# Eight-step chunks and float32 matmuls in a state-space layer and in neighbourhood attention

## The chip, the cores and the metric

One core of a Trainium2 chip runs the whole kernel as one launch. The metric is the device time of that launch in microseconds (us), as the median of the timed runs. Engines are called as the profile does: PE (matmul), PEld (its weight loads), DVE (vector), ACT (scalar), POOL (GpSimd) and SP (which issues most DMAs).

## The reference, cut to what matters

One layer over 512 latent tokens and 256 context tokens of width 1024. A combined projection feeds a convolution branch, a state-space branch and an attention branch; their outputs are gated, merged and projected, and an MLP follows. Everything is float32.

```python
def s5_latent_states(ux, s5p, h0_f, h0_b):        # 32 groups of 16 channels, 64 complex states, two directions
    h_f = diag_scan(lam_bar[0], s5_drive(ux, b_bar[0])) + jnp.exp(lam_dt[0] * steps) * h0_f[:, None]
    h_b = diag_scan(lam_bar[1], jnp.flip(s5_drive(ux, b_bar[1]), 1)) + jnp.exp(lam_dt[1] * steps) * h0_b[:, None]
    return h_f, jnp.flip(h_b, 1)
...
def s5_output(u, h_f, h_b, c_mat, d_skip, w_glu_a, w_glu_b):
    y = jnp.real(jnp.einsum('blgp,gnp->blgn', h_f, c_mat[0]) + jnp.einsum('blgp,gnp->blgn', h_b, c_mat[1]))
    y = y.reshape(u.shape).astype(u.dtype) + d_skip * u
    g = jax.nn.gelu(y)
    return (g @ w_glu_a) * jax.nn.sigmoid(g @ w_glu_b)
...
    # attention, 8 heads of 64: each grid row of 64 queries sees a window of 8 x 16 and all 256 context keys
    s_loc = jnp.einsum('bqhd,bwkhd->bhqwk', q_r, k_r).astype(jnp.float32) * scale + bias
    s_loc = jnp.where(key_in[:, None, :], s_loc, NEG_INF)
    s_ctx = jnp.einsum('bqhd,bchd->bhqc', q_r, kch).astype(jnp.float32) * scale
    p = jax.nn.softmax(jnp.concatenate([s_loc.reshape(...), s_ctx], axis=-1), axis=-1)
    return jnp.einsum('bhqwk,bwkhd->bqhd', p_loc, v_r) + jnp.einsum('bhqc,bchd->bqhd', p[..., n_loc:], vch)
```

The scan has a period: over a chunk of some steps the state is multiplied by a power of lam_bar and gets a sum of the inputs of these steps, so it can be run over chunks, with small matrices for what goes on within one.

## The kernel before

Large products are made of **units** (list in `unit_list`, line 37): cg and xb (convolution), uc (context input of the state-space layer), ga, cv, gb, gc (gates and convolution output), q, k, v, then lb, la (GLU of the state-space layer), na (attention output), wo and the MLP's m1 and m2. A unit has 1 MB or half of it of weights; blocks of two halves stream from DRAM on SP's queue (`fetch`, 130; two blocks ahead). To keep float32 accuracy each operand is split into two reduced-precision parts (F32R), hi and lo: ACT casts, DVE subtracts (`wsplit`, 161; `split`, 90), and a product is three matmuls, hi-hi, hi-lo and lo-hi (`mm3`, lines 99 to 101). A unit is 24 matmuls of 512 columns; k and v have 24 more of 256 columns for the context; uc has 24 of 256.

`slot` (1172) makes one unit: it splits the weights of the unit two places on, pumps the **generators** that are open (a piece of side work each), makes half of the products, pumps again and makes the other half. The framework then orders the instructions of each engine from a simulated timeline; the state-space generator has high priority (`ahead`). Generators: `gen_par` (230), powers of the state-space parameters on [128, 32] tiles; `gen_ctx` (506); `gen_mod` (1128), late modulation columns on POOL, ACT and DVE; then `gen_s5a`, `gen_s5b` and attention.

**S5A** (`gen_s5a`, 528) runs in eight batches of four groups. With chunks of four steps it makes the matrices E (inputs to chunk states) and CA (states to outputs), 256 wide for a batch; six products or sums each on POOL and DVE (`prod`, 536). E goes to DRAM, E and the masked C are split, and 16 short matmuls per batch (580, 581) give lag matrices (kps, kev). At the end these go through DRAM twice to become Toeplitz blocks: KF_d and KB_d are written, read as kf and kb (600), added on POOL (603) and written as K_d.

**S5B** (class at 612, `gen_s5b` at 758) moves pairs of groups through a pipeline, two pieces to a step, 16 pairs. Piece A: `load` (E and, every second pair, u in eight DMAs), `load2` (CA, K), `scan` of the pair before (four scans of 192 chunks: 64 of context, 128 of latent tokens), `states` (12 split matmuls of 192 columns), `transp` (E transposed on PE), `back1`, `rot1`, `back2`. Piece B: `rot2`, `outp` of two pairs before (18 split matmuls of 128 columns; the K part uses 64 rows), then the splits of E and u, the sine `table`, and the splits of h, CA and K. DVE does scans, rotations and lo parts; POOL rr, v, h and one lo part; ACT casts and sines. Results go to Y_d in DRAM.

**Attention** (class at 798) works on four pairs of heads times four tiles of 128 queries. Its pool of tiles needs the memory of S5B, so S5B must be through: the run (1218 to 1237) lets it end before q1, and q0, k0 and v0 may lie beside its last steps. `scores` (830) takes hi and lo of k stacked on 128 rows against doubled q, then a 64-row matmul for q's lo part: eight matmuls a tile. DVE adds the bias (842) and takes the maximum (843), ACT the exponential (850), DVE scales, PE transposes eight blocks (863), ACT and DVE split them (pth, ptl), and `values` (869) needs 24 matmuls with 64-wide weights, both heads on output partitions 0 to 63.

Of the kernel before, what the change touches and what calls it, by code (L numbers as in the profile page):

```python
# [53 lines left out]
def stream_list():  # L54
    """Halves in the order in which they are read: start, then units with the late modulation tiles."""
# [20 lines left out]
def trunk(tc, xT, ctxT, cond, vecs, wst, s5p, s5bc, dmat, biasA, outT):  # L76
# [5 lines left out]
    def f(ap):  # L82
        return ap.bitcast(F32)
# [20 lines left out]
    with es:  # L104
# [120 lines left out]
        # =====================================================================  # L225
        # S5: parameters, then per batch of four groups E, CA and the lag matrices
        # =====================================================================
        s5 = {}

        def gen_par(pool, keep):  # L230
            n_sl = [0]
            prm = pool.tile([128, 40, G], F32, name="prm")
# [48 lines left out]
            pr, pi = [None] * 5, [None] * 5  # L281
            pr[1], pi[1] = sl(), sl()
            V.tensor_tensor(pr[1], r1, cs, op=MUL)
            V.tensor_tensor(pi[1], r1, sn, op=MUL)
            ph = keep.tile([128, G], F32, name="ph")
            V.tensor_scalar(ph, tht, 4.0 * 0.15915494309189535, None, op0=MUL)
            V.tensor_scalar(k, ph, ROUND, ROUND, op0=ADD, op1=SUB)
            V.tensor_tensor(ph, ph, k, op=SUB)
            r4 = keep.tile([128, G], F32, name="r4")
            V.tensor_tensor(r4, r1, r1, op=MUL)  # L290
            V.tensor_tensor(r4, r4, r4, op=MUL)
            yield

            t1, t2 = sl(), sl()

            def cmul(orr, oi, ar, ai, br, bi):
                V.tensor_tensor(t1, ai, bi, op=MUL)
                V.tensor_tensor(t2, ai, br, op=MUL)
                V.tensor_tensor(orr, ar, br, op=MUL)
                V.tensor_tensor(oi, ar, bi, op=MUL)  # L300
                V.tensor_tensor(orr, orr, t1, op=SUB)
                V.tensor_tensor(oi, oi, t2, op=ADD)

            for i, (x, y) in {2: (1, 1), 3: (2, 1), 4: (2, 2)}.items():
                pr[i], pi[i] = sl(), sl()
                cmul(pr[i], pi[i], pr[x], pi[x], pr[y], pi[y])
                yield
            # q = (lam_bar - 1) / lam
            den, nr, qr, qi = sl(), sl(), sl(), sl()
# [4 lines left out]
            V.tensor_scalar(nr, pr[1], 1.0, None, op0=SUB)  # L314
            V.tensor_scalar(t2, lim, -1.0, None, op0=MUL)
            yield
            nl = sl()
            V.tensor_copy(nl, t2)
            cmul(qr, qi, nr, pi[1], lre, nl)
            V.tensor_tensor(qr, qr, den, op=MUL)  # L320
            V.tensor_tensor(qi, qi, den, op=MUL)
            yield
            dr, di = [qr], [qi]
            for i in range(1, 4):
                dr.append(sl())
                di.append(sl())
                cmul(dr[i], di[i], qr, qi, pr[i], pi[i])
                yield
            CF = {n: keep.tile([128, G, 4], F32, name="CF" + n) for n in ("cr", "nci", "ncr", "ar", "ai")}
            for s in range(4):  # L330
                for lo_, hi_, e, c in ((0, 64, 3 - s, s + 1), (64, 128, s, 4 - s)):
                    sel = slice(lo_, hi_)
# [279 lines left out]
        class S5B:  # L612
# [37 lines left out]
            def transp(self, q):  # L650
                ps = pa(f"etps{q}")[:, :256].rearrange("p (c m) -> p c m", c=2)
                for c in range(2):
                    PE.transpose(ps[:, c], self.t["eb", q][:, c], ident)
# [840 lines left out]
```

## Time and profile before

| what | us |
|---|---|
| timed runs (three), lowest, median, highest | 1111.8, 1113.29, 1119.03 |
| the profiled execution: span from the first to the last instruction | 1117.5 |
| PE busy in the span | 1028.6 (92%) |
| DVE busy | 749.1 (67%) |
| ACT busy | 473.8 (42%) |
| POOL busy | 324.2 (29%) |

The profiled execution has no time of its own apart from its span, which is 4 us above the median of the timed runs. A busy PE is not PE at its peak: matmuls overlap, so start-to-start distances tell the rate, and durations don't. PEclk is the granted clock of PE as a share of full speed.

### The profile page before, as it was taken

To read this page: it belongs to the slowest core of one execution; us is meant where nothing else is said; L and a number is where in the kernel's file an instruction comes from. 1 tells how busy PE (TensorE), PEld (TensorE's weight loads), DVE (VectorE), ACT (ScalarE), POOL (GpSimd) and SP (SyncE) were. 2 spreads that over 40 slices of the span, in tenths; PEclk is the share of its full clock that TensorE was granted. 3 is DMA by queue.
4 is the path that set the end of the run, shared out by engine and by line. 5 is a ranking of instruction groups with operands and counts; after the bars stand their busy time and mean duration, and the time that the engine had idled before them with its cause. 6 is when DMAs were issued, how large, how long until landed. Compare 5 with 4: busy or idle time off the path is not lost.

```text
span 1117.5 us, 14237 instructions
## 1 busy us (share of the span) xinstructions
PE 1028.6 (92%) x5350; PEld 848.0 (76%) x5350; DVE 749.1 (67%) x1084; ACT 473.8 (42%) x843; POOL 324.2 (29%) x254
## 2 busy tenths in 40 slices
PE   4669978989898898899999999999999999999997
PEld 3448777767676676777887778899888888888887
DVE  8999899628979989977658787756443223443322
ACT  5336543216444535545556554434432112433211
POOL 2771565216877878761010010000000000000000
PEclk9789989998888898899999999999999999999999
DMA  7544156395334353333224355522232323232202
GB/s 267 188 188 151 49 196 217 125 139 182 103 90 142 120 163 133 137 126 138 97 98 146 132 187 172 215 76 81 109 113 76 113 76 113 79 110 88 101 1 76
DMA packets 62760, 142.81 MB, mean 128 GB/s; under 512 B 18194, under 2 KB 40978, under 8 KB 50212
## 3 DMA queue, kind: packets, MB, share of 16 engines
q1 hardware_dynamic: 60788, 138.75, 37.8%
q10 hardware_dynamic: 1904, 3.16, 0.9%
q8 instruction: 42, 0.69, 0.2%
q14 instruction: 26, 0.21, 0.1%
HBM read 125.96 MB, written 15.93 MB: 127 GB/s over the span
## 4 chain that ended last, share of the span: by engine, by line
PE 58%; POOL 9%; DVE 7%; DMA 3%; issue 3%; SPq 2%; ACT 1%; DVEq 0%; POOLq 0%; ACTq 0%
PE m L99 10%; PE m L100 10%; PE m L101 10%; DVE v L711 2%; PE sps L840 2%; POOL v L703 2%; PE ptps L863 1%; PE sps L839 1%; PE wo L100 1%; PE wo L99 1%; PE wo L101 1%; POOL h L726 1%; PE ops L99 1%; POOL h L723 1%; POOL h L725 1%
## 5 line engine op out<-in xcount | busy, mean ns | idle before, releaser
L174 DVE TENSOR_TENSOR wl<-raw,wh 128x1024 fp32r<-128x1024 f32 x144 | 188.9, 1313 | 142.5 <-ACT wh L171 140.6
L171 ACT CAST wh<-raw 128x1024 fp32r<-128x1024 f32 x144 | 150.7, 1047 | 251.1 <-PE m L100 151.1
L99 PE MATMUL m<-rg,wh 128*128 128x512 f32 (+1 forms) x480 | 184.2, 385 | 0.0
L101 PE MATMUL m<-rg,wl 128*128 128x512 f32 (+1 forms) x480 | 183.9, 384 | 0.0
L101 PEld LDWEIGHTS m<-rg,wl 128*128 128x128 f32 x480 | 90.1, 188 | 19.0
L99 PEld LDWEIGHTS m<-rg,wh 128*128 128x128 f32 x480 | 90.0, 188 | 18.7
L100 PE MATMUL m<-rg,wh 128*128 128x512 f32 (+1 forms) x256 | 96.4, 378 | 0.0
L100 PE MATMUL m<-actl,wh 128*128 128x512 f32 x224 | 87.8, 392 | 0.0
L1134 POOL TENSOR_TENSOR junk<-raw,silx 128x1024 f32<-128x1024 f32 x16 | 43.0, 2684 | 138.3 <-DMA raw<-in_wst_dram 138.3
L711 DVE TENSOR_TENSOR_SCAN v<-r,v 128x192 f32<-128x192 f32 x64 | 53.5, 882 | 10.0 <-POOL v L703 7.5
L438 POOL TENSOR_TENSOR prod<-raw,silc 128x1024 f32<-128x1024 f32 x16 | 47.1, 2968 | 35.0 <-ACT prod L447 23.5
L100 PEld LDWEIGHTS m<-rg,wh 128*128 128x128 f32 x256 | 48.0, 188 | 8.6
L100 PEld LDWEIGHTS m<-actl,wh 128*128 128x128 f32 x224 | 42.0, 188 | 9.8
L1089 DVE SCALAR_TENSOR_TENSOR fg<-m,mod,fg 128x512 f32<-128x512 f32 x14 | 10.5, 752 | 52.8 <-PE m L101 52.8
L92 ACT CAST rg<-relu 128x512 fp32r<-128x512 f32 (+1 forms) x36 | 20.3, 575 | 38.6 <-DVE relu L1082 38.6
L93 DVE TENSOR_TENSOR actl<-relu,rg 128x512 fp32r<-128x512 f32 (+1 forms) x36 | 22.3, 633 | 18.5 <-ACT rg L92 18.5
L723 POOL TENSOR_TENSOR h<-A 64x256 f32<-64x256 f32 x16 | 19.7, 1231 | 44.1 <-DVE A L717 44.1
L92 ACT CAST hh<-h 128x512 fp32r<-128x512 f32 x16 | 9.9, 618 | 52.8 <-POOL h L726 52.7
L100 PE MATMUL wo<-rg,wh 128*128 128x256 f32 (+1 forms) x104 | 32.0, 309 | 0.0
L436 DVE SCALAR_TENSOR_TENSOR junk<-raw,silx 128x1024 f32<-128x1024 f32 x16 | 31.8, 1988 | 0.0
L101 PE MATMUL wo<-rg,wl 128*128 128x256 f32 (+1 forms) x104 | 31.7, 306 | 0.0
L99 PE MATMUL wo<-rg,wh 128*128 128x256 f32 (+1 forms) x104 | 31.6, 307 | 0.0
(484 smaller groups left out, 2943.6 us busy)
## 6 DMA issues: line engine op xcount, KB each, us to landing
raw<-in_wst_dram SPq DMA_DIRECT2D x94, 1024.0 KB, 4.9
E_d<-e SPq DMA_DIRECT2D x8, 512.0 KB, 2.9
u<-U_d SPq DMA_DIRECT2D x64, 48.0 KB, 2.1
fg<-in_xT_dram SPq DMA_DIRECT2D x4, 512.0 KB, 5.8
raw<-in_wst_dram SPq DMA_DIRECT2D x4, 512.0 KB, 7.4
U_d<-un SPq DMA_DIRECT2D x4, 512.0 KB, 3.8
bc<-in_s5bc_dram ACTq DMA_DIRECT2D x8, 256.0 KB, 3.0
eb<-E_d SPq DMA_DIRECT2D x16, 128.0 KB, 2.8
```

Of the source, the lines that this page charges most:

```text
L92: S.copy(hi, src)
L99: PE.matmul(ps, a[0], b[0], start=start, stop=False)
L100: PE.matmul(ps, a[0], b[1], start=False, stop=False)
L101: PE.matmul(ps, a[1], b[0], start=False, stop=stop)
L171: S.copy(a, src)
L174: V.tensor_tensor(b, src, f(a), op=SUB)
L436: jins[d] = V.scalar_tensor_tensor(junk, w, 1.0, silx, op0=MUL, op1=MUL, accum_out=modx[:, h[1]:h[1] + 1])
L438: P.tensor_tensor(pr, w, silc, op=MUL)
L703: P.tensor_tensor(v[:, :, 0], A[:, :, 0], A[:, :, 1], op=SUB)
L711: V.tensor_tensor_scan(v[:, g, c], r4, v[:, g, c], 0.0, op0=MUL, op1=ADD)
L723: P.tensor_tensor(h[0:64, 0], A[0:64, :, 0], A[0:64, :, 1], op=ADD)
L1134: P.tensor_tensor(junk, half(h), silx, op=MUL)
```

## The change

**State-space layer.** Chunks have eight steps instead of four, so there are 32 + 64 = 96 of them instead of 192, and groups go through S5B by four instead of two: eight steps. All its matmuls take float32 operands directly; the splits are gone. `gen_par` makes powers 1 to 8 in wider operations. S5A's products are twice as wide; PE transposes E there, before E_d is written. The lag matrices are written once, to one table KT_d, from which each step reads its Toeplitz block. u is stored forward only; the backward direction reads it with a negative step, as a second matmul into the right half of the array (output partitions 64 to 127).

**Attention.** q, k, v and the probabilities stay float32. A head's scores use its own 64 rows of q and k, so the two heads use the upper and lower half of the array's rows; in `values` they use the left and the right half of its columns. The bias tile has zeros for the context keys, and one DVE instruction adds and takes the maximum. S5B now has to end before q0.

```diff
@@ gen_s5a
+                e1 = pool.tile([128, 2, 512], F32, tag="e1", bufs=2, name=f"e1{b}")
+                c1 = pool.tile([128, 2, 512], F32, tag="c1", bufs=1, name=f"c1{b}")
...
+                nc.sync.dma_start(C_d[b], c1)
                 yield
-                ebh = pool.tile([128, 512], F32R, tag="ebh", name=f"ebh{b}")
-                ebl = pool.tile([128, 512], F32R, tag="ebl", name=f"ebl{b}")
-                split(ebh, ebl, e1[:, 0:2].rearrange("p c m -> p (c m)"))
-                nc.sync.dma_start(E_d[b], e1)
...
+                        PE.transpose(ps[:, 2 * g + c], e1[:, c, 128 * g:128 * g + 128], ident)
+                for g in range(4):
+                    for c in range(2):
+                        PE.matmul(kps[:, g], e1[:, c, 128 * g:128 * g + 128], cm[:, 4 * c + g], start=c == 0, stop=c == 1)
+                et = pool.tile([128, 8, 128], F32, tag="et", bufs=1, name=f"et{b}")
+                S.copy(et, ps)
+                nc.sync.dma_start(E_d[b], et)
+                S.copy(kev[:, 4 * b:4 * b + 4], kps)
...
+            for s in range(8):
+                if s < 7:
+                    nc.sync.dma_start(KT_d[:, :, 16 * (14 - s):16 * (15 - s)].rearrange("g n m -> n g m"), kev[16 * s:16 * s + 16, :, 0:16])
+                nc.sync.dma_start(KT_d[:, :, 16 * (7 - s):16 * (8 - s)].rearrange("g n m -> n g m"), kev[16 * s:16 * s + 16, :, 16:32])
...
-            P.tensor_tensor(kf, kf, kb, op=ADD)
-            yield
-            nc.sync.dma_start(K_d, kf)
@@ class S5B
             def load(self, q):
+                et = self.tl("et", q, [128, 8, 128], bufs=2)
+                nc.sync.dma_start(et, E_d[q])
+                u = self.tl("u", q, [128, 4, 128], bufs=4)
+                for s in range(8):
+                    nc.sync.dma_start(u[16 * s:16 * s + 16], U_d[s, 64 * q:64 * q + 64].rearrange("(g n) m -> n g m", n=16))
             def load2(self, q):
+                ca = self.tl("ca", q, [128, 2, 4, 128], bufs=1)
+                nc.sync.dma_start(ca.rearrange("p c g m -> p (c g m)"), C_d[q].rearrange("p c m -> p (c m)"))
+                ks = self.tl("ks", q, [128, 4, 128], bufs=1)
+                for s in range(8):
+                    nc.sync.dma_start(ks[16 * s:16 * s + 16], KT_d[4 * q:4 * q + 4, :, 16 * (7 - s):16 * (7 - s) + 128].rearrange("g n m -> n g m"))
...
             def states(self, q):
+                for g in range(4):
                     for c in range(2):
-                        a = 2 * c + g
-                        mm3(ps[:, g, 192 * c:192 * c + 192], (eh[:, a], el[:, a]), (uh[:, g], ul[:, g]), True, True)
+                        w = et[:, 2 * g + c]
+                        o = ps[:, g // 2, g % 2, c]
+                        PE.matmul(o[0:64], w[:, 0:64], u[:, g, 0:96], start=True, stop=True, skip_group_check=True)
+                        PE.matmul(o[64:128], w[:, 64:128], u[:, g, 127:31:-1], start=True, stop=True, skip_group_check=True)
...
             def outp(self, q):
+                for g in range(4):
+                    PE.matmul(ps[:, g], ks[:, g], u[:, g, 32:96], start=True, stop=False)
                     for c in range(2):
+                        PE.matmul(ps[:, g], ca[:, c, g], h[:, c, g], start=False, stop=c == 1)
+                y = late["y"].tile([128, 4, 64], F32, tag="yd", bufs=1, name=f"y{q}")
+                S.copy(y, ps)
+                for s in range(8):
+                    nc.sync.dma_start(Y_d[64 * q:64 * q + 64, s].rearrange("(g n) m -> n g m", n=16), y[16 * s:16 * s + 16])
...
@@ gen_s5b
-            for t in range(-2, 19):
+            for t in range(-2, 11):
...
-                if ok(t - 2):
-                    sb.outp(t - 2)
+                if ok(t - 1):
+                    sb.outp(t - 1)
                 if ok(t + 1):
-                    sb.esplit(t + 1)
-                    sb.usplit(t + 1)
                     sb.table(t + 1)
-                if ok(t - 1):
-                    sb.hsplit(t - 1)
@@ class ATT, scores
+                    for c0, c1, o in ((k0, k0 + nk, 256 - nk), (512, 768, 256)):
+                        for h in range(2):
+                            r = slice(64 * h, 64 * h + 64)
+                            PE.matmul(ps[:, h, o:o + c1 - c0], q[r, 128 * i:128 * i + 128], k[r, c0:c1], start=True, stop=True)
...
+                        V.tensor_tensor_reduce(out=sl, in0=sl, in1=bia[n][:, h, 256 - nk:512], scale=1.0, scalar=-3.0e38,
+                                               op0=ADD, op1=ALU.max, accum_out=mx[:, h:h + 1])
@@ transp, values
-                    split(pth, ptl, pt)
+                    S.copy(pt[:, 0], ps[:, 0])
+                    V.tensor_copy(pt[:, 1], ps[:, 1])
...
+                    for t, (vt, rows) in enumerate(tiles):
+                        for h in range(2):
+                            r = slice(64 * h, 64 * h + 64)
+                            PE.matmul(ops[r], v[:rows, vt, r], pt[:rows, h, t], start=t == 0, stop=t == 3, skip_group_check=True)
@@ run
-            if UNITS[i] == ("q", 1):
+            if UNITS[i] == ("q", 0):
                 pump()
                 continue
```

## Rows read from the trace of the kernel before

**Rows 1.** Chain that ended last, share of the span by engine.

```profile
PE 58%; POOL 9%; DVE 7%; DMA 3%; issue 3%; SPq 2%; ACT 1%; DVEq 0%; POOLq 0%; ACTq 0%
```

**Rows 2.** Windows: us, then busy time (x instructions) of each engine, PEclk, DMA share, GB/s.

```profile
98.70:170.00 71.30, 63.23 (x323) 53.24 (x322) 66.62 (x135) 34.23 (x54) 39.45 (x43) 0.93 0.49 158
170.00:258.00 88.00, 77.21 (x386) 62.94 (x387) 50.86 (x71) 26.83 (x45) 30.61 (x33) 0.92 0.65 152
258.00:430.00 172.00, 150.53 (x768) 121.39 (x767) 155.61 (x183) 87.57 (x202) 131.48 (x112) 0.88 0.42 132
430.00:490.00 60.00, 52.98 (x282) 43.36 (x281) 51.71 (x66) 26.29 (x57) 46.68 (x36) 0.85 0.39 135
490.00:684.00 194.00, 193.51 (x1187) 154.92 (x1187) 136.39 (x185) 109.67 (x206) 28.22 (x12) 0.97 0.39 134
684.00:706.00 22.00, 22.00 (x99) 18.16 (x98) 21.00 (x31) 10.89 (x15) 0.00 (x0) 1.00 0.67 223
```

**Rows 3.** Chain in order of time, one step of S5B: start us, us, what.

```profile
278.79 3.22 DVE v L711 x4
...
289.37 2.13 POOL v L703
291.53 3.29 DVE v L711 x4
```

**Rows 4.** One source line, the scans: duration ns min/median/max, first and last start.

```profile
L711 DVE TENSOR_TENSOR_SCAN v<-r,v x64: 522/546/2683, 266.7 to 484.0; 128x192 f32<-128x192 f32 x64
```

**Rows 5.** Timeline of PE, transposes and value matmuls: start us, us, what.

```profile
546.58 0.27 PE L863 MATMUL ptps<-ident,pr 128*128 128x128 f32 x1
...
546.75 0.28 PE L863 MATMUL ptps<-ident,pr 128*128 128x128 f32 x1
...
547.09 0.22 PE L100 MATMUL ops<-ptl,vh 128*64 128x128 f32 x1
547.15 0.22 PE L101 MATMUL ops<-pth,vl 128*64 128x128 f32 x1
```

**Rows 6.** Timeline of PE around a float32 matmul of 256 columns.

```profile
745.41 0.59 PE L366 MATMUL nps<-n_0dg,ones 128*128 128x256 f32 x2
...
745.96 0.28 PE L101 MATMUL wo<-rg,wl 128*128 128x256 f32 x1
```

**Rows 7.** Timeline of PE, float32 matmuls of one column.

```profile
1099.53 0.36 PE L354 MATMUL nps<-ones,ss 128*128 128x1 f32 x2
1099.75 0.36 PE L354 MATMUL nps<-ones,sq 128*128 128x1 f32 x2
```

**Rows 8.** Chain in order of time, from S5A to S5B.

```profile
231.88 10.35 DMA kb<-KB_d
...
256.73 2.09 DMA u<-U_d
```

**Rows 9.** Groups by line, POOL, the products of S5A: busy us, mean ns, idle before.

```profile
L565 POOL TENSOR_TENSOR e<-e,ta 128x256 f32<-128x256 f32 x8 | 8.9, 1108 | 0.0
...
L540 POOL TENSOR_TENSOR e<-bc,CFnci 128x256 f32<-128x256 f32 x8 | 6.5, 810 | 28.3 <-DMA bc<-in_s5bc_dram 17.2 <-issue 10.4 <-DVE ebl L93 0.7
```

**Rows 10.** Groups by line, DVE, the first and last split of S5B.

```profile
L93 DVE TENSOR_TENSOR ul<-u,uh 128x384 fp32r<-128x384 f32 x16 | 15.1, 949 | 0.4 <-DMA u<-U_d 0.4
...
L93 DVE TENSOR_TENSOR kl<-ks,kh 64x128 fp32r<-64x128 f32 x16 | 10.9, 680 | 0.0
```

**Rows 11.** One source line, SP's issues of u: duration ns min/median/max.

```profile
L641 SPq DMA_DIRECT2D u<-U_d x64: 302/424/1539, 252.0 to 401.2; - x64
```

**Rows 12.** Timeline of PE, score matmuls (64*128 has 64 rows), with and without units.

```profile
527.79 0.28 PE L839 MATMUL sps<-k,q 128*128 128x256 f32 x1
...
528.87 0.25 PE L839 MATMUL sps<-k,q 128*128 128x192 f32 x1
...
554.42 0.38 PE L839 MATMUL sps<-k,q 128*128 128x256 f32 x1
...
555.04 0.39 PE L839 MATMUL sps<-k,q 128*128 128x256 f32 x1
```

More of the change, by code (lines that the diff above doesn't have):

```diff
@@ L231, in gen_par @@
             n_sl = [0]
-            prm = pool.tile([128, 40, G], F32, name="prm")
+            prm = pool.tile([128, 14, G], F32, name="prm")
             def sl():
@@ L280, in gen_par @@
             V.tensor_scalar(cs, cs, -2.0, 1.0, op0=MUL, op1=ADD)
[L281 to L284, printed above, removed]
+            wk = tp.tile([128, 768], F32, tag="vt", bufs=1, name="parw")
+            PW = wk[:, 0:512].rearrange("p (c s g) -> p c s g", c=2, s=8)
+            qn, cl, q = (wk[:, 512 + 64 * i:576 + 64 * i].rearrange("p (c g) -> p c g", c=2) for i in range(3))
@@ L285, in gen_par @@
+            CF = {n: keep.tile([128, G, 8], F32, name="CF" + n) for n in ("cr", "nci", "ar", "ai")}
+            tm = [CF[n].rearrange("p g s -> p (g s)") for n in ("ar", "ai")]
+            V.tensor_tensor(PW[:, 0, 0], r1, cs, op=MUL)
+            V.tensor_tensor(PW[:, 1, 0], r1, sn, op=MUL)
             ph = keep.tile([128, G], F32, name="ph")
-            V.tensor_scalar(ph, tht, 4.0 * 0.15915494309189535, None, op0=MUL)
+            V.tensor_scalar(ph, tht, 8.0 * 0.15915494309189535, None, op0=MUL)
@@ L296, in cmul @@
-            def cmul(orr, oi, ar, ai, br, bi):
-                V.tensor_tensor(t1, ai, bi, op=MUL)
-                V.tensor_tensor(t2, ai, br, op=MUL)
+            def cmul(out, A, B, n, sel=slice(None)):
+                (ar, ai), (orr, oi) = A, out
+                m = ar.shape[0]
+                br, bi = (x[:, None, :].to_broadcast([m, n, G]) for x in B)
+                t0, t1 = (t[sel, 0:n * G].rearrange("p (s g) -> p s g", s=n) for t in tm)
+                V.tensor_tensor(t0, ai, bi, op=MUL)
+                V.tensor_tensor(t1, ai, br, op=MUL)
@@ L307, in gen_par @@
+            pair = lambda t, e, sel=slice(None): (t[sel, 0, e], t[sel, 1, e])
+            for n in (1, 2, 4):
+                cmul(pair(PW, slice(n, 2 * n)), pair(PW, slice(0, n)), pair(PW, n - 1), n)
                 yield
-            den, nr, qr, qi = sl(), sl(), sl(), sl()
+            t1, den = sl(), sl()
             V.tensor_tensor(t1, lre, lre, op=MUL)
@@ L576, in gen_s5a @@
+                yield
+                ps = pa(f"etps{b}").rearrange("p (a m) -> p a m", a=8)
+                kps = pss(f"kps{b}")[:, :128].rearrange("p (g m) -> p g m", g=4)
                 for g in range(4):
                     for c in range(2):
-                        eh, el = (t[:, 256 * c + 64 * g:256 * c + 64 * g + 64] for t in (ebh, ebl))
-                        cg = cm[:, 4 * c + g]
-                        PE.matmul(kps[:, g], eh, cg, start=c == 0, stop=False)
-                        PE.matmul(kps[:, g, 0], el, cg[:, 0], start=False, stop=c == 1)
@@ L820, in gen @@
                 bia = {}
+                bt = [late["paf"].tile([128, 2, 512], F32, name=f"bt{e}") for e in range(2)]
+                for t in bt:
+                    P.memset(t[:, :, 256:512], 0.0)
                 def load_bias(n):
@@ L1225, in trunk @@
         s5b_cm.__exit__(None, None, None)
-        while UNITS[i] != ("q", 1):
+        keep_cm.__exit__(None, None, None)
+        while UNITS[i] != ("q", 0):
             slot(i)
@@ L1240, in load_g @@
             for j in range(4):
-                yd = (tp_att, late["y"])[j % 2].tile([128, 4, 128], F32, tag="yd", bufs=1, name=f"yd{j}")
+                yd = (tp_att, late["y"])[j % 2].tile([128, 8, 64], F32, tag="yd", bufs=1, name=f"yd{j}")
                 nc.sync.dma_start(yd, Y_d[128 * j:128 * j + 128])
```

348 lines of the change are left out of this document (117 added, 231 removed).

## The prediction

> **What bounds the kernel now.** I first read the chain that ended last, by engine [rows 1]: PE holds 58% of the span, POOL 9%, DVE 7%. So the matrix engine is the limit, but not everywhere. The stage windows say where [rows 2]. From 490 us on PE is busy in every microsecond, at a clock of 0.97 to 1.00. From 98.7 to 490 us it is busy for 88 to 89% of the time, at a granted clock between 0.85 and 0.93 (means of its two levels, 1.2 and 2.4 GHz), while DVE (90% of 258 to 430) and POOL (76%) are close to full. There the chain itself runs through DVE and POOL: one step of the state-space pipeline goes scan, POOL, POOL, next scan, from 278.79 to 291.53, that is 12.7 us [rows 3], and 16 steps lie between 266.7 and 484.0 [rows 4], 13.8 us each.
>
> How much PE time that costs, I work out against the dense rate. The four units "na" (24 matmuls of 512 columns each) take 22.00 us [rows 2]: 5.5 us a unit, 0.229 us a matmul, and half of that for 256 columns. From 98.7 to 684 us stand 36 plain units from cg to gc (198), four uc (11), q 22, eight k and v of 8.25 (66) and eight lb and la (44): 341 us of 585. The other 244 us, window by window: 16 (to 170), 22 (to 258), 84 (to 430), 38 (to 490), 84 (to 684). The last 84 is attention, 5.2 us for each of 16 tiles. Of the first 38, some 8 are 128 short kps matmuls at about 0.06 [rows 5], and 30 are lost. Of the 122 from 258 to 490, about 48 are the state-space matmuls (16 pairs; 12 at 192 columns near 0.1, 18 at 0.06, two transposes at 0.11 and some switching: 3 us), so 74 us, 4.6 a step, is PE waiting or running at the low clock.
>
> **The change, part by part.** A float32 matmul of 256 columns shows as two records, from 745.41 to 745.96 with one split matmul of 0.115 in between [rows 6]: 0.43 us, four times the dense time of a column. With one column and 128 weights it takes 0.22 [rows 7], the price of its two weight loads; for 64 weights I take half, 0.11, an estimate. So a matmul costs the larger of 0.22 (or 0.11) and 1.7 ns a column, where three split matmuls cost 1.35 ns a column.
>
> *S5A, eight batches.* Removed: the split of cm and of E, and the kf/kb round trip after it, from 231.88 to the first u load at 256.73, 25 us in which the pipeline does not start [rows 8]. Added: all products are twice as wide. Six POOL instructions of a batch take 0.81 to 1.11 us, 5.4 in all [rows 9]; doubled, 10.9, so POOL needs 87 us where it needed 44. That lengthens S5A by about as much as the round trip took: it ends near 230 instead of 256. DVE's six products double too, against the two splits and one addition that go: some 20 us more over the stage, beside POOL. PE: 8 transposes at 0.11 and 8 float32 matmuls at 0.22 make 2.6 us a batch, 21 in all, for 8 before: +13. I leave the stalls of this stage at 30 us (15 if the shorter tail helps, 60 if POOL holds PE up).
>
> *S5B, from 16 steps to 8.* Each step now has four groups and half as many chunks (96 for 192). DVE's scans are 8 of 96 columns for 4 of 192: 2.2 us at 0.546 [rows 4] as before, products and rotations as before; the four split subtractions, 0.95 to 0.68 us [rows 10], 3.5 a step, are gone; so are one on POOL and the casts on ACT. So a step costs DVE and POOL somewhat less than a pair did, and there are 8, not 16: about half of the work of the window in which they were full. Scan, back-rotation, h on POOL, v on POOL remain as the loop: 9 to 13 us a step, hence 8 steps and a lead of two, some 110 to 120 us, from 230 to 350. PE has enough to hide it: gb and gc alone are 88 us. What is late next is SP: a step issues 26 DMAs (et, eight u, ca, eight ks, eight Y) where two pair steps issued 18, at 0.424 us each [rows 11]: 11 us a step. Each waits in order, in front of the weight blocks; two blocks of weights lie ahead, so I price this into the stall. PE's own work: 16 matmuls of 96 columns at 0.16 and 12 at 0.22 are 5.2 us a step, 42 in all, or 31 if the left and right halves of the array run beside each other; I take 37 (before 48). For stalls I take 3.5 us a step, 28 in all: less than 4.6, as the splits between the stages are gone, but 0 and 45 are possible.
>
> *Attention.* Each tile has 4 score matmuls of 256 columns at 0.43, 1.7 us, for 8 split ones; values 8 of 128 columns at 0.215, 1.7 us, for 24 at 0.06; transposes and the share of v 1.1 as before. A switch from 128 rows to 64 and back costs 0.39: a full, a 64-row and two unit matmuls take 1.08 instead of 0.69, and without unit matmuls between them 0.62 instead of 0.23 [rows 12]. Before there were four such runs in a tile, 1.6 us; now one to four, I take two, and 0.2 for the half tiles. One after another: 5.5 us, 88 for 16 tiles, no gain over 84. If the two heads, on separate halves, run together as far as a pair of records in order lets them (5 slots for 8 records, 9 for 16): 4.1 us, 65. Nothing in the trace runs on both halves at once, so I take the middle, 77. The Trainium skill, "TensorEngine Tiling (Array Packing)", Key Properties, says that tiles operate independently, their loads and matmuls in parallel; by that rule the sum would use 65. Its other rule there, that a change of tiling mode drains the engine, is what [rows 12] shows for rows.
>
> DVE (add and maximum in one, no ptl) and ACT (no pth) lose work here; PE is the limit, so that gives nothing by itself. The removed q and k splits and the smaller un copies are beside PE as well. q0, k0, v0 move behind S5B: no cost of their own, but S5B's tail no longer has them as cover; it doesn't need them if it ends near 350.
>
> **Sum to the start of na:** 98.7 + 209 (cg to gc) + 21 + 30 (S5A) + 37 + 28 (S5B) + 132 (q to la) + 77 (attention) = 633 against 684: 51 us less. From there nothing changes. The profiled execution spans 1117.5 us, 4 more than the median of the timed runs (1113.3); I take the difference from the median: 1062 us, with 1035 to 1090 for this case.
>
> **Rivals.** *The halves overlap and S5B is hidden wholly.* S5B 31 and a stall of 10, attention 65: another 36 us, 1026. For: the loops put the two halves next to each other, and DVE and POOL lose half of their load. Against: no row shows an overlap, and unit matmuls were put between the score matmuls before [rows 12]. By the Trainium skill's rule of independent tiles (same section) this is the expected outcome; the trace is silent on it.
>
> *S5 stays the limit.* POOL's doubled products make a batch 13 us and SP's 26 issues a step 14, PE's order is fixed beforehand and waits for both: stalls of 50 in S5A and 45 in S5B, 37 more: 1099, and 1113 if each is some 7 us worse. For: POOL at 76%, the in-order SP queue. Against: the round trip and half of the steps are gone.
>
> *Slower: switching between halves and the whole array.* If unit matmuls alternate with each float32 matmul on a half, as they did with the scores, and column halves drain the array like row halves, 16 matmuls a step in S5B and 12 a tile in attention pay 0.39: 320 of them, 125 us, 12 of which I have counted. With all halves in series (1078) it decides from a third of them on; at two thirds it is 1078 + 75 = 1153. Against: 64-wide value matmuls alternate with 128-wide transposes at 0.17 a pair, which is the 0.11 and the 0.06 they need alone [rows 5], so columns (on the left half) cost no drain now. By the Trainium skill's rule (same section) a switch of mode would always drain; the trace agrees for rows, not for columns.
>
> **Chances.** Forecast 0.54; overlap 0.17; S5 still the limit 0.18, of which 0.08 within 1% of before; slower 0.11. About 1% is what a measurement of this kernel tells from no change. Faster by more: 0.54 + 0.17 + 0.10 = 0.81; within 1%: 0.08; slower: 0.11. Range 1015 to 1106: below it little of the overlap case is left out, above it the slower one and part of the S5 one.
>
> **What would show it.** Right: the chain has no kb load and POOL kf; 64 scans of 96 columns between about 240 and 350; gc ends near 425 with a clock above 0.9, no state-space matmul after it; na starts near 633. Score matmuls as 128 records at about 0.2; starts of the two heads closer than that mean overlap. Wrong: PE gaps before kps or states with POOL or SP as releaser; S5B beyond 430; gaps of 0.2 us around 64-column matmuls; attention, less its units, over 90 us.

## The result, and the profile after

| | before | after |
|---|---|---|
| timed runs, median (lowest to highest), us | 1115.44 (1111.8 to 1119.03) | 1063.08 (1061.63 to 1064.7) |
| profiled execution, span, us | 1117.5 | 1062.3 |
| first matmul of na, us | 684 | 628.9 |
| from there to the end, us | 433.5 | 433.4 |

The ratio is 0.9528, 95% interval 0.9497 to 0.9559 (four runs each): 52 us less. The forecast was 1062. All of the gain lies ahead of na, as predicted.

The chain that ended last, by engine; it answers to [rows 1].

```profile
PE 71%; DVE 3%; DMA 2%; SPq 2%; issue 1%; POOL 0%; ACT 0%; DVEq 0%; ACTq 0%; POOLq 0%
```

POOL's 9% and half of DVE's 7% have left the chain. The windows of after, cut where units begin (ga at 179.3, gb at 284.6, the last gc and q at 418.6, the first scores at 444, na at 628.9); columns as in [rows 2].

```profile
98.70:179.30 80.60, 70.87 (x363) 60.66 (x362) 71.18 (x91) 34.58 (x51) 51.44 (x42) 0.92 0.47 142
179.30:284.60 105.30, 94.22 (x562) 77.85 (x561) 83.00 (x91) 27.83 (x42) 65.41 (x49) 0.95 0.61 181
284.60:418.60 134.00, 121.43 (x681) 102.20 (x680) 66.52 (x109) 36.55 (x58) 52.34 (x49) 0.92 0.61 189
418.60:444.00 25.40, 25.40 (x136) 21.71 (x134) 11.29 (x12) 10.14 (x15) 6.68 (x3) 1.00 0.57 209
444.00:628.90 184.90, 184.90 (x1080) 136.41 (x1080) 117.62 (x221) 88.22 (x171) 27.79 (x10) 1.00 0.40 138
```

The windows show the exchange. The stretch to gb's start became longer, 284.6 where [rows 2] had 258: from start to start it now holds 23.5 us of S5A's transposes and short matmuls where it held 8.2, and the first 12.6 us of S5B's matmuls. S5A itself became longer too: its last E is stored at 238.5 instead of 210.9. From gb's start to gc's end it is 134 us instead of 172, and the window from 430 to 490, in which S5B still ran, is gone. DVE is busy for 66.5 of 134 us (half) where it was at 90%, POOL for 39% instead of 76%. Less their units (121.5, 88 and 132.6 us at the dense rates), the stretches cost 64.4 us to gb's start, 46 to gc's end, 77.7 from there to na.

The scans [rows 4], and two timelines of PE: S5B's state matmuls (lines 653 and 654 are the left and the right half of the array; the first two and the last two of 16 pairs of records without a gap, the work of 16 matmuls), and a tile of attention.

```profile
L678 DVE TENSOR_TENSOR_SCAN v<-r,v x64: 325/328/1171, 262.0 to 369.0; 128x96 f32<-128x96 f32 x64
```

```profile
257.50 0.30 PE L653 MATMUL stps<-u,et 128*64 128x96 f32 x1
257.51 0.30 PE L654 MATMUL stps<-u,et 128*64 128x96 f32 x1
257.63 0.25 PE L653 MATMUL stps<-u,et 128*64 128x96 f32 x1
257.64 0.25 PE L654 MATMUL stps<-u,et 128*64 128x96 f32 x1
...
258.71 0.25 PE L653 MATMUL stps<-u,et 128*64 128x96 f32 x1
258.71 0.25 PE L654 MATMUL stps<-u,et 128*64 128x96 f32 x1
258.79 0.25 PE L653 MATMUL stps<-u,et 128*64 128x96 f32 x1
258.80 0.25 PE L654 MATMUL stps<-u,et 128*64 128x96 f32 x1
...
464.13 1.13 PE L786 MATMUL sps<-k,q 64*128 64x256 f32 x8
465.19 0.80 PE L827 MATMUL ops<-pt,v 64*64 64x128 f32 x6
465.92 0.33 PE L812 MATMUL ptps<-ident,pr 128*128 128x128 f32 x1
466.18 0.43 PE L827 MATMUL ops<-pt,v 128*64 128x128 f32 x2
466.54 0.33 PE L812 MATMUL ptps<-ident,pr 128*128 128x128 f32 x1
466.80 0.43 PE L827 MATMUL ops<-pt,v 128*64 128x128 f32 x2
...
474.15 1.09 PE L827 MATMUL ops<-pt,v 128*64 128x128 f32 x14
475.17 1.03 PE L786 MATMUL sps<-k,q 64*128 64x192 f32 x8
476.13 1.09 PE L812 MATMUL ptps<-ident,pr 128*128 128x128 f32 x8
```

What no row of before could show is here: records of the left and the right half start 0 to 10 ns apart in these rows, and the next pair 0.08 us later. Each float32 matmul is two records. Starts alone do not prove that the halves work beside each other; what that saves is measured below, with both heads on one half. The four score matmuls (eight records) take 1.06 us, from 464.13 to 465.19, where 4 x 0.43 would be 1.72. Seven value matmuls (14 records) take 1.02 us (474.15 to 475.17). But from 466.18 to 466.80 a value matmul and a transpose that alternate take 0.62 us, where the same take 0.15 and 0.11 in rows of their own kind (1.02 / 7, and 0.85 / 8 from 476.13 to the next matmul at 476.98). Before, such a pair took 0.17 [rows 5].

S5A's chain, a piece of it in order of time.

```profile
204.25 3.11 DMA C_d<-c
...
207.38 3.10 DVE c L538 x2
...
215.42 4.14 DMA C_d<-c
...
219.59 3.11 DVE c L538 x2
...
228.11 2.13 POOL e L556
...
230.29 0.47 PE etps L573
230.76 0.43 PE cv L100
```

The C part of a batch (tile c1) has one buffer, so a batch's products on DVE can't start until the C before has been stored; DVE sat idle for that three times in the stage, 3.2 us in all. PE waits behind that for POOL's e, and comes back at the lower of its two clock levels (granted clock 0.50 from 230.3 to 235.4): the cv matmul at 230.76 takes 0.43 us instead of 0.23.

The same stretch in the timelines of DVE and of POOL:

```profile
207.38 1.40 DVE L538 TENSOR_TENSOR c<-bc,CFar 128x512 f32<-128x512 f32 x1 [0.82 <-DMA C_d<-c]
208.70 1.78 DVE L538 TENSOR_TENSOR c<-bc,CFai 128x512 f32<-128x512 f32 x1
...
213.97 0.69 DVE L538 TENSOR_TENSOR ta<-bc,CFar 128x512 f32<-128x512 f32 x1
214.70 0.69 DVE L566 TENSOR_TENSOR c<-c,ta 128x512 f32<-128x512 f32 x1
```

```profile
207.17 1.06 POOL L538 TENSOR_TENSOR ta<-bc,CFcr 128x512 f32<-128x512 f32 x1
208.31 1.62 POOL L563 TENSOR_TENSOR e<-e,ta 128x512 f32<-128x512 f32 x1
...
211.36 2.03 POOL L538 TENSOR_TENSOR e<-bc,CFcr 128x512 f32<-128x512 f32 x1
215.54 1.55 POOL L538 TENSOR_TENSOR ta<-bc,CFnci 128x512 f32<-128x512 f32 x1 [2.15 <-DVE c L566]
```

From 213.4 to 215.5 POOL runs nothing, and there a product on DVE takes 0.69 us. Beside POOL's work it takes 1.40 to 1.78. So the two slow each other, and a busy DVE or POOL in S5A is in part one that waits for the other.

### The profile page after: what moved, and what is told of

It reads as the page before. It is cut to its first block, busy times and chain, and to the rows that moved or that the text cites. A ratio compares the mean times of both kernels' runs of the same rounds, so it can differ in the third digit from the quotient of the medians.

```text
span 1062.3 us, 13475 instructions
## 1 busy us (share of the span) xinstructions
PE 988.0 (93%) x5222; PEld 810.9 (76%) x5222; DVE 635.5 (60%) x959; ACT 385.4 (36%) x616; POOL 251.5 (24%) x173
## 4 chain that ended last, share of the span: by engine, by line
PE 71%; DVE 3%; DMA 2%; SPq 2%; issue 1%; POOL 0%; ACT 0%; DVEq 0%; ACTq 0%; POOLq 0%
PE m L99 10%; PE m L100 10%; PE m L101 10%; PE ops L827 3%; PE sps L786 2%; PE ptps L812 2%; PE wo L100 1%; PE wo L99 1%; PE wo L101 1%; PE gc L99 1%; PE gc L100 1%; PE gc L101 1%; PE yps L702 1%; PE gb L101 1%; PE gb L99 1%; DVE v L678 1%
## 5 line engine op out<-in xcount | busy, mean ns | idle before, releaser
L174 DVE TENSOR_TENSOR wl<-raw,wh 128x1024 fp32r<-128x1024 f32 x144 | 193.7, 1346 | 161.8 <-ACT wh L171 159.8
L1064 POOL TENSOR_TENSOR junk<-raw,silx 128x1024 f32<-128x1024 f32 x16 | 45.2, 2824 | 183.4 <-DMA raw<-in_wst_dram 183.4
L442 POOL TENSOR_TENSOR prod<-raw,silc 128x1024 f32<-128x1024 f32 x16 | 47.2, 2974 | 35.1 <-ACT prod L451 23.5
L1068 DVE SCALAR_TENSOR_TENSOR jk<-raw,silx 128x1024 bf16<-128x1024 f32 x16 | 21.5, 1345 | 43.2 <-DMA raw<-in_wst_dram 43.2
L678 DVE TENSOR_TENSOR_SCAN v<-r,v 128x96 f32<-128x96 f32 x64 | 27.1, 490 | 10.7 <-POOL v L670 10.7
L827 PE MATMUL ops<-pt,v 128*64 128x128 f32 (+1 forms) x256 | 32.5, 288 | 0.0
```

The source lines that it names most:

```text
L174: V.tensor_tensor(b, src, f(a), op=SUB)
L442: P.tensor_tensor(pr, w, silc, op=MUL)
L678: V.tensor_tensor_scan(v[:, g, c], r8, v[:, g, c], 0.0, op0=MUL, op1=ADD)
L827: PE.matmul(ops[r], v[:rows, vt, r], pt[:rows, h, t], start=t == 0, stop=t == 3, skip_group_check=True)
L1064: P.tensor_tensor(junk, half(h), silx, op=MUL)
L1068: V.scalar_tensor_tensor(jk, half(h), 1.0, silx, op0=MUL, op1=MUL, accum_out=modx[:, i:i + 1])
```

## The experiments

Ten kernels ran. Each is compared with the kernel before on its own chip, so ratios compare across groups; the profiled executions' own stretches differ by 1 to 3 us where the code is the same (gb starts between 280.6 and 284.6 in the six kernels whose S5A is that of the change).

**The state-space part alone.** Attention, q, k and v of the kernel before, with S5B ending before q1.

```diff
-                            PE.matmul(ps[:, h, o:o + c1 - c0], q[r, 128 * i:128 * i + 128], k[r, c0:c1], start=True, stop=True)
...
-            if UNITS[i] == ("q", 0):
+            if UNITS[i] == ("q", 1):
```

> The new state-space layer with the attention of before (splits, q1 as the boundary). Theory: the gain is the state-space layer's; attention takes 78 us of PE after the change and took 84 before, so this kernel should be 6 us (4 to 9) slower than the changed one: 1069. Rival: the overlap of the halves carries a large part of the gain, since the float32 attention would be no faster than the split one without it; then this kernel stands 18 us or more above the changed one: 1081 or more.

Measured: 1072.89 us, ratio 0.9597 (0.9583 to 0.9612), na at 633.9. So the state-space layer brings 4.0% and attention the last 0.7%, some 8 us (0.0069 of 1115), close to the 6 of the theory and far from 18. Of na's start 5 us show; the last value matmuls stand between the na units here, and from gc's end to the first wo matmul it is 243.0 us instead of 232.0.

**Heads one after the other in attention.** The two loops are exchanged in scores and in values.

```diff
-                    for c0, c1, o in ((k0, k0 + nk, 256 - nk), (512, 768, 256)):
-                        for h in range(2):
+                    for h in range(2):
+                        for c0, c1, o in ((k0, k0 + nk, 256 - nk), (512, 768, 256)):
...
-                    for t, (vt, rows) in enumerate(tiles):
-                        for h in range(2):
+                    for h in range(2):
+                        for t, (vt, rows) in enumerate(tiles):
```

> The changed kernel with the two heads one after the other in scores and values (all matmuls of a head first), so that neighbours use the same half of the array. Theory of the overlap: a score tile then takes 3 x 0.43 instead of 2 x 0.43 us or more, values 7 x 0.215 instead of 4 x 0.215, 1.1 to 1.5 us more in each of 16 tiles: 18 to 24 us slower than the changed kernel, 1081 to 1087. Rival: records of the two halves only start close to each other and the array works them off one by one: within 3 us of the changed kernel.

Measured: 1069.09 us, ratio 0.9569 (0.9546 to 0.9592): some 5 us more than the changed kernel (0.0041, within the two intervals; from gc's end to na 217.5 us instead of 210.2), not what the theory expected. Its timeline says why.

```profile
470.69 1.58 PE L827 MATMUL ops<-pt,v 128*64 128x128 f32 x16
472.20 1.03 PE L786 MATMUL sps<-k,q 64*128 64x192 f32 x8
```

The scores still take 0.96 us (to 473.16, the next matmul), as in after: PE paired head 0's and head 1's matmuls although two of head 0 come first in its order. The two matmuls of 192 columns, one of each head, start 13 ns apart at 472.20, ahead of head 0's 256 columns (472.63), which stand between them in that order. The values, four of a head in a row, are paired only in part: 1.51 us for eight (470.69 to 472.20), 0.19 each instead of 0.15; the first four records start alone, some 0.11 apart, and only with the fifth does the other head's first one start (both at 471.18). The edit did not take the overlap away, so it could not price it; a second design had to.

**Both heads on the same half.**

```diff
-                            r = slice(64 * h, 64 * h + 64)
+                            r = slice(0, 64)
...
-                    ops = pss(f"ops{n}")[:, :128]
+                    ops = pss(f"ops{n}")[:64, :256].rearrange("p (h m) -> p h m", h=2)
...
-                                PE.matmul(ops[r], v[:rows, vt, r], pt[:rows, h, t], ...)
+                                PE.matmul(ops[:, h], v[:rows, vt, r], pt[:rows, h, t], ...)
```

> The changed kernel with both heads of a tile on the same half of the array: the scores of both slots use rows 0 to 63 (head 0's scores are computed twice, head 1's are left out), and the values of both heads use output partitions 0 to 63, head after head. Amount of matmul work and column switches are the same or fewer. Theory (attention gains because the two halves run beside each other): 4 score matmuls take about 1.9 us instead of 1.06, 8 value matmuls about 1.8 instead of 1.0, so 16 tiles cost some 27 us more, less up to 5 for fewer column switches: na starts 20 to 27 us later than 628.9, time 1083 to 1090, ratio about 0.975. Rival (the float32 matmuls are cheap by themselves, as their operands need no splits, and the halves add nothing): no change within 5 us, 1060 to 1068, ratio 0.950 to 0.957.

Besides, the values go head after head, as in the run before, which the diff above does not show.

Measured: 1078.53 us, ratio 0.9663 (0.9635 to 0.9691), na at 646.4. Against after that is 0.0135, 15 us; by na's start in the profiled executions 17.5, by the stretch from gc's end to na 19.4 (229.6 for 210.2). The rival (no change) fell. The theory's 20 to 27 was somewhat high, but the records are close to what it said: its timeline, then the groups of this run, then those of after.

```profile
471.28 1.96 PE L828 MATMUL ops<-pt,v 128*64 128x128 f32 x16
473.17 1.78 PE L787 MATMUL sps<-k,q 64*128 64x192 f32 x8
```

```profile
L828 PE MATMUL ops<-pt,v 128*64 128x128 f32 (+1 forms) x256 | 40.2, 285 | 0.0
L787 PE MATMUL sps<-k,q 64*128 64x256 f32 (+1 forms) x128 | 32.5, 383 | 0.0
```

```profile
L827 PE MATMUL ops<-pt,v 128*64 128x128 f32 (+1 forms) x256 | 32.5, 288 | 0.0
L812 PE MATMUL ptps<-ident,pr 128*128 128x128 f32 x128 | 22.7, 286 | 0.0
L786 PE MATMUL sps<-k,q 64*128 64x256 f32 (+1 forms) x128 | 21.9, 394 | 0.0
```

Eight value matmuls take 1.89 us on one half (471.28 to 473.17), 0.24 each instead of 0.15; busy time rises by 18.3 us over the 16 tiles. Without the overlap attention would have cost some 93 to 97 us instead of 77.7, more than the 83.5 of before (194.0 in [rows 2] less 110.5 for its units).

**Values and transposes in separate runs.**

```diff
-                            PE.matmul(ops[r], v[:rows, vt, r], pt[:rows, h, t], ...)
+                            self.lv = PE.matmul(ops[r], v[:rows, vt, r], pt[:rows, h, t], ...)
...
-                        pt = transp(n - 1, prev)
+                        with (tc.issue_after(self.lv.ins) if n > 1 else nullcontext()):
+                            pt = transp(n - 1, prev)
```

> The changed kernel with the transposes of a tile ordered behind the last value matmul of the tile before, so that the two do not alternate; 101 instead of 139 changes between whole array, row halves and column halves in attention's order, all that go between columns and whole. Theory (a change to 64 columns and back drains PE at about 0.1 us each way): 38 changes fewer are 4 us, na starts near 625, time about 1059, ratio 0.949. Rival (the 0.1 us belongs to the loads of the weights and not to the change of columns, or values now wait for their probabilities): no gain, 1062 to 1066, ratio 0.952 or more.

Measured: 1058.92 us, ratio 0.9486 (0.946 to 0.9512), na at 622.4. By the ratios alone it can't be told from after; by the stretch from gc's end to na it can: 206.7 us (415.7 to 622.4) for 210.3. Its groups, to be read against those of after above:

```profile
L827 PE MATMUL ops<-pt,v 128*64 128x128 f32 (+1 forms) x256 | 26.1, 285 | 0.0
...
L812 PE MATMUL ptps<-ident,pr 128*128 128x128 f32 x128 | 18.3, 277 | 2.3 <-DVE pr L802 2.3
```

Both fall though the work is the same. Summed from start to start, values go from 29.0 to 23.9 us and transposes from 15.9 to 12.7; scores and lb take back 4.2 (20.2 to 22.6 and 23.6 to 25.4), and 3.6 reach na, near the 4 expected. So alternating has its price; some of it moves to the matmuls that now stand next to the runs. Not all of the values' 5.1 us need be the change of columns: 19 of them stood alone between other work in after and are in runs here, and there a value matmul takes 0.15 us instead of the 0.24 of one half, 0.09 less. The run does not separate the two. The transposes, which are never paired, fall by 3.2 us all the same.

**The output and Toeplitz DMAs on another queue.**

```diff
-                    nc.sync.dma_start(ks[16 * s:16 * s + 16], KT_d[...])
+                    nc.scalar.dma_start(ks[16 * s:16 * s + 16], KT_d[...])
...
-                    nc.sync.dma_start(Y_d[...], y[16 * s:16 * s + 16])
+                    nc.scalar.dma_start(Y_d[...], y[16 * s:16 * s + 16])
```

> The changed kernel with the 8 ks loads and the 8 Y stores of each state-space step issued by ACT instead of SP. Theory: SP's 26 issues of 0.42 us and their order set the state-space step (13 us from scan to scan); with 10 left the step falls to about 10 us, the last scan starts some 25 us earlier, and PE's stalls between 284.6 and 418.6 us (about 20) fall by 5 to 10 us: 1053 to 1058. Rival: that chain lies beside the gb and gc units and PE waits for other things: 1060 to 1066, with the scans earlier. If ACT's issues delay the weight casts: slower, 1070.

Measured: 1068.32 us, ratio 0.9563 (0.9547 to 0.9579), na at 629.0. Not faster. The last scan starts at 353.7 instead of 369.0, and na starts where it did: so far the rival held (1067 by the ratio, just above its range). But the run also moved a wait:

```profile
401.02 0.66 PE L700 MATMUL yps<-u,ks 128*128 128x64 f32 x2 [8.32 <-ACT tgc L953]
```

Ahead of the last step's outputs PE is idle for 8.3 us, longer than any of its waits in S5B in after (5.7). What releases it, ACT's tgc, starts only at 400.38: before 399.33 ACT's engine sat idle for 11.7 us, while its queue issued and waited for the ks loads and Y stores that it now has. Taking 16 of 26 issues a step from SP brings nothing when ACT gets them; what SP's issues cost by themselves stays open.

**Two buffers for c1.**

```diff
-                c1 = pool.tile([128, 2, 512], F32, tag="c1", bufs=1, name=f"c1{b}")
+                c1 = pool.tile([128, 2, 512], F32, tag="c1", bufs=2, name=f"c1{b}")
```

> The changed kernel with two buffers for c1 in S5A, so that the products of a batch need not wait until the C_d write of the batch before has landed. Theory: the chain goes C_d write 3.1 to 4.1 us, products, C_d write; without that wait the batch loses 2 to 3 us and the stage some 15 us, of which PE gets 5 to 15: 1048 to 1058. Rival: DVE and POOL are the limit of the stage (DVE waited only 3.2 us for these writes): within 3 us of the changed kernel.

Measured: 1051.46 us, ratio 0.9405 (0.939 to 0.9421): 12 to 14 us below the changed kernel. The size is as expected, the place is not, so the hit is luck. The unit rows of this run, and a window of it from gb's start to gc's end, to be read against the third one of after:

```profile
L99 PE MATMUL gb<-rg,wh x64: 388/389/632, 280.2 to 342.7; 128*128 128x512 f32 x64
...
L99 PE MATMUL na<-rg,wh x32: 389/389/392, 617.0 to 638.1; 128*128 128x512 f32 x32
```

```profile
280.20:401.00 120.80, 116.06 (x657) 96.89 (x657) 72.91 (x113) 36.34 (x58) 54.76 (x50) 0.96 0.63 194
```

The store of the last E in S5A is issued at 238.5, to the tenth where it was in after, and gb starts at 280.2, at the edge of the spread of that start. So c1's buffer was in S5A's chain, but S5A is no shorter without it: DVE is as busy as before (153.3 us to gb's start, 154.2 in after). The gain lies between gb's start and gc's end: PE is idle for 4.7 of 120.8 us, where it was for 12.6 of 134, and its clock is 0.96 instead of 0.92. There the planned order has changed with c1: S5B's matmuls, first to last, enclose 423 unit matmuls instead of 396, and the last step's outputs fall behind gc, for which some is paid back (from gc's end to na 216 us instead of 210). How the buffer of one stage comes to change the order of the next was not followed further.

**S5A's tiles all separate**, and **with the values in a run** as well. The first adds to the last kernel:

```diff
-                ta = pool.tile([128, 2, 512], F32, tag="ta", name=f"ta{b}")
+                ta = pool.tile([128, 512], F32, tag="ta", name=f"ta{b}")
+                tv = pool.tile([128, 512], F32, tag="tv", name=f"tv{b}")
...
-                et = pool.tile([128, 8, 128], F32, tag="et", bufs=1, name=f"et{b}")
+                et = pool.tile([128, 8, 128], F32, tag="et", bufs=2, name=f"et{b}")
```

> The run with two buffers for c1, and besides separate scratch tiles for POOL and DVE in the S5A products and two buffers for the transposed E. Theory (S5A's stall comes from waits between its engines for shared tiles: POOL waits for DVE on the shared scratch, PE's transposes wait for POOL's E): gb starts 3 to 10 us before 280.2, na 3 to 10 before 617.0, time 1042 to 1049, ratio 0.932 to 0.938. Rival (with c1 doubled, POOL's and DVE's own work sets S5A, and what an S5A piece saves S5B loses again to its loads): 1050 to 1053, ratio 0.939 to 0.942.

Measured: 1049.33 us, ratio 0.9397 (0.9369 to 0.9426), the same as with c1 alone, although S5A's last E is now stored at 234.7 and not at 238.5. The rival held.

> Both of the last two runs in one kernel, as a candidate for the best version. If the column changes cost 0.1 us each way and do not overlap S5A, it takes 4 us less than the run with the freed S5A tiles, 1038 to 1046; if not, the same time as that run.

Measured: 1045.57 us, ratio 0.9366 (0.9338 to 0.9395), na at 611.4 instead of 615.1. The 3.7 us of the ordered values add to what the kernel without them had gained. This is the fastest kernel of the study, 18 us below the changed one.

**One step more of lead for S5B's loads**, on top of it.

```diff
-                u = self.tl("u", q, [128, 4, 128], bufs=4)
+                u = self.tl("u", q, [128, 4, 128], bufs=5)
...
-                ca = self.tl("ca", q, [128, 2, 4, 128], bufs=1)
+                ca = self.tl("ca", q, [128, 2, 4, 128], bufs=2)
...
-                ks = self.tl("ks", q, [128, 4, 128], bufs=1)
+                ks = self.tl("ks", q, [128, 4, 128], bufs=2)
...
-                if ok(t - 1):
-                    sb.load2(t - 1)
+                if ok(t):
+                    sb.load2(t)
```

> The candidate above, with two buffers for CA and the Toeplitz block and three SP queue places earlier for them: they are loaded one step ahead (u has five buffers for it), so a step's output matmuls no longer wait for loads that could only start when the step before had freed their tile. Theory (the rest of S5B's stall, 9.7 us of PE waiting for u and ks and some lost clock behind it, is the loads' buffers): gc ends 5 to 10 us earlier than in the candidate, time 1035 to 1041, ratio 0.928 to 0.934. Rival (SP's 26 issues a step at 0.42 us set the pace, whatever the buffers, and they now also stand in front of the weight blocks): no gain, ratio 0.934 or more.

Measured: 1087.48 us, ratio 0.9744 (0.9715 to 0.9774): 42 us slower than without it, which neither theory had. Windows of this run (columns as above), and SP's issues of weight blocks between 300 and 366 us, all there are.

```profile
300.00:320.00 20.00, 14.60 (x133) 12.55 (x131) 13.79 (x30) 4.11 (x9) 12.99 (x15) 0.93 0.47 131
320.00:340.00 20.00, 11.01 (x88) 10.32 (x88) 12.27 (x28) 3.51 (x8) 13.94 (x17) 0.50 0.50 132
340.00:360.00 20.00, 13.71 (x62) 13.39 (x63) 5.58 (x14) 0.74 (x2) 4.75 (x6) 0.50 0.47 123
```

```profile
361.32 0.85 SPq L142 DMA_DIRECT2D raw<-in_wst_dram  x2
```

From 320 to 360 PE has only S5B to do: it runs no unit matmul, is busy for 62% of the time, and has the lower clock (0.50). The first weight block after 300 us is issued at 361. In PE's order S5B's matmuls enclose 92 unit matmuls (21 us of cover at the dense rate), where the kernel without the edit has 423 (97 us). The loop itself is as fast as forecast for it: scans begin at 279.6, 291.2, 301.1, 313.9, 323.1 and 332.9 in its chain, 9 to 13 us a step.

**The buffers without the earlier place** tells apart what did it.

```diff
-                if ok(t):
-                    sb.load2(t)
+                if ok(t - 1):
+                    sb.load2(t - 1)
```

(u has four buffers again.)

> The candidate with two buffers for CA and the Toeplitz block alone; they are loaded where they were. In PE's order, S5B's matmuls from the first to the last now enclose 188 unit matmuls, where the candidate has 423 and the run that loads a step ahead has 92. Theory (that run was slow because the single buffers had held the steps apart: without that wait the scheduler packs the eight steps together, PE has no unit work to do meanwhile, and no weight block is issued past them): between the two, some 15 to 25 us above the candidate, 1058 to 1072, ratio 0.949 to 0.960. Rival (it was the earlier place of the loads that put 9 issues a step in front of the weight blocks): no worse than the candidate, ratio 0.934 to 0.940.

Measured: 1078.94 us, ratio 0.9655 (0.962 to 0.969): 33 us slower than without the buffers, so the place of the loads isn't what cost most. With 423, 188 and 92 unit matmuls inside S5B the ratio is 0.937, 0.966 and 0.974. The direction and the order are the theory's, its 15 to 25 us was too little. The traces bear it out: without a unit matmul PE goes 29.8 us here (343.2 to 373.0) and 58.7 us with the earlier loads (309.0 to 367.7), where the kernel without the edit has no such gap over 7.5 us between 280 and 420; and no weight block is issued here between 287.6 and 366.2. That the ordering of the instructions, and not some contention, does it is still argued from these counts; the cover was not varied without the buffers.

## Why the prediction was right

By its own terms, in us, to the start of na:

| term | predicted | measured |
|---|---|---|
| S5A, PE and stall | 21 + 30 = 51 | 64.4 - 12.6 of early S5B = 52 |
| S5B, PE and stall | 37 + 28 = 65 | 46 + 12.6 = 59 |
| attention less its units | 77 | 77.7 |
| units at the dense rate, cg to gc and q to la | 209 + 132 | 209.5 + 132.6 |
| start of na | 633 | 628.9 |

The 12.6 are the start-to-start sums of the state and output matmuls ahead of gb. By such sums S5A splits into 23.5 and 28.3, S5B into 45 and 13: in S5B the matmuls cost more than forecast and the stalls less.

**S5A.** POOL took 75.9 us for its 48 instructions (six rows of 11.0 to 15.1 us) where 87 were forecast from doubled widths. S5A ended at 238.5 and not at 230. The step that failed is "some 20 us more over the stage, beside POOL": DVE's products don't simply lie beside POOL's; where they meet, DVE's take 1.40 to 1.78 us instead of 0.69, and POOL's up to 2.03 instead of 1.06. The Trainium skill, "SBUF — State Buffer", "SBUF: two separate sides", says that DVE and GpSimd share a pair of ports, held for the whole instruction by one of GpSimd, or against one that reads SBUF by an operation of DVE with two SBUF inputs, while the other is fully blocked; the trace agrees as far as durations show it, with 0.69 against 1.40 to 1.78 us. On top, POOL waited for DVE on the shared scratch tile (8.6 us), and PE for POOL's e (13.5 us). Doubling c1 alone left the end where it was, separate tiles brought 4 us; that is what two engines taking turns would show, but it is argued, as no run moved the work to another engine. POOL's costliest row, to be read against [rows 9]:

```profile
L556 POOL TENSOR_TENSOR e<-e,ta 128x512 f32<-128x512 f32 x8 | 15.1, 1882 | 0.6
```

The stall term of 30 had room for it, and the K round trip's 25 us [rows 8] were spent again in S5A, as forecast.

**S5B.** Half the steps, and with them less than half of the work: DVE is busy for 66.5 us from gb's start to gc's end, where [rows 2] had 155.6 in the same units (in the whole kernel, S5B's own instructions with their splits take 65 us of DVE instead of 174). No run separates the longer chunks from the dropped splits. A step's eight scans take 2.6 us (0.328 each), not the 2.2 forecast: half the columns took more than half the time. Scans ran from 262 to 369 (240 to 350 forecast), gc ended at 418.6 (425). From one step's first scan to the next's it took 8.5 to 13.7 us five times, near the 9 to 13 forecast, then 29.9 and 17.5. With the loads a step ahead all seven take 9 to 13. So the loop could go as fast as forecast, and single buffers, SP's order or the planned order of PE, which were not told apart, spread its last steps over gb and gc; that was the cheaper way. The prediction's "PE has enough to hide it" holds only while the unit work lies between the steps.

**Attention.** The number is right, its working is not: two errors that went opposite ways met at 77, which is luck. "In the middle, 77" stood for partial overlap. In fact the halves overlap nearly as far as the prediction's own full count (4.1 us a tile, 65) has it: four score matmuls take 1.06 us where it counted 1.08, a value matmul in a run 0.15 where it counted 0.12 and one half takes 0.24. The Trainium skill, "TensorEngine Tiling (Array Packing)", Key Properties, says that tiles work independently; the trace agrees, with 0 to 10 ns between the two halves' records in the rows shown. And a cost that the prediction had argued away came on top: "columns cost no drain now". Where value matmuls alternate with transposes, the pair takes 0.62 us. On one half a value matmul takes 0.24 (1.89 / 8), a transpose 0.11, so some 0.27 go into the two changes, 0.14 each; PE's order has 139 changes of rows or columns in attention, 19 us if each costs that much, an estimate. With 65 less the 12 that it had in it for changes, plus 19, the count comes to 72; the other 6 were not traced. The Trainium skill's other rule in that section, that a change of tiling mode drains the engine, fits this loss. The row from which the prediction took columns to be free [rows 5] has value matmuls in the split form, not in float32.

**The rivals.** Full overlap was right for the halves, but S5B was not hidden wholly, so 1026 was not reached; with freed S5A tiles and ordered values it is 1046. S5 staying the limit: the long S5A came, S5B did not stay. The slower rival had a real mechanism, but 0.27 for two changes instead of 0.39, 70 such pairs in attention instead of the 320 it counted in all. In S5B a step's 16 matmuls on halves stand in one run, or 14 and 2, and its 12 output matmuls use the whole array.

## What to carry to other kernels

Two float32 matmuls on two halves of the array can cost little more than the time of one, so what counts is where the whole-array work falls between them: group matmuls of one shape, and keep the loops over halves adjacent. A tile that the chain names need not be the limit: doubling c1 left its stage as long. And where DVE's and POOL's operations slow each other, as they did here, splitting the work over both saves less than it seems. Last, a wait can be what keeps a side chain spread under the main work: before removing one, count the main engine's instructions that lie between the side chain's first and last.

## What was not expected of the hardware

Program order between the halves did not hold the pairing: with two score matmuls of head 0 ahead of two of head 1, the eight records took 0.96 us as before, while with four value matmuls of a head in a row, each took 0.19 us, between 0.15 (pairs) and 0.24 (one half). In the values the second half's first matmul started together with the third of the first half; in the scores, with the first. So a half ran ahead of two matmuls of the other that come before it in order, but not of four.

Columns cost nothing to change in the split form (0.17 a pair [rows 5]) and 0.14 us a change in float32. The run with both heads on the left half alternates a few values with transposes too; it shows the same steps (0.36 and 0.26 us), so the right half isn't the reason. Whether it is the float32 form or something else of these matmuls was not tried.
